# A fused decoder block: where the sums of the down projection's weights are made

## The chip, the cores and the metric

The kernel runs on one core of one Trainium2 chip. The metric is the device time of one launch in microseconds. The kernel before took 697.74, 702.74 and 703.54 us in three runs, median 702.74 us. One further execution was profiled. It took 699.71 us, and its span from the first to the last instruction is 697.9 us.

## What is computed

One layer of a residual decoder block, with 512 tokens of width 1024, everything in float32. `h` is a gained RMS norm of `x`, modulated by columns of `c_act @ ada_w`.

```python
h = rms_norm(x, norm1_g) * (1 + scale1) + shift1
q, k, v, p, g_attn, g_pool = split(h @ w_in)
attn = moba_attention(rms_norm(q), rms_norm(k), v, rel_bias)      # 8 heads of 64
pool = multiscale_pool(p) ...                                     # windows 2, 4, 8, 16
merged = sigmoid(g_attn) * (attn @ w_branch_attn) + sigmoid(g_pool) * (pool @ w_branch_pool)
x = x + gate1 * (merged @ w_out)
h2 = rms_norm(x, norm2_g) * (1 + scale2) + shift2
u = causal_dwconv(h2 @ w_up, conv_w, conv_b)
u_g, u_v = split(u)
x = x + gate2 * ((silu(u_g) * u_v) @ w_down)                      # w_down is 2816 x 1024
```

## The kernel before, in words

**Precision.** Each float32 operand of a large product is split into a high part, rounded by ScalarE (`hi_of`, L114), and a low part, a subtraction on VectorE (L124). Three matmuls (`mm3`, L133 to L135; `more`, L139 to L141) stand for one product.

**Stages, in order.** (1) `x` is normed and transposed. The columns of `ada_w` come as 512 KB tiles and are summed with `c` (`ada_sum`, L207). For each of eight 128-wide slices k of the width, the p and q projections accumulate `h_k` into eight banks of PSUM (`mm3s`, L146 and L149). Slice k needs two ada tiles, summed, and half of a tile of p and of q weights. (2) The k and v projections (`tok_proj`). (3) The norms of q and k, the transposes (`stacks`, L550) and per head the attention, with the sixteen gate projections filled in between (`gate_stream`). (4) The branches and `w_out`, then the second norm per token tile (`out_norm`). (5) The up projection, 22 channel pairs j, each with its convolution, SiLU and product on ScalarE and VectorE. (6) The down projection.

**Down by seven products.** The down projection multiplies 2x2 blocks with seven products instead of eight. It needs four blocks of `w_down` as they are (b11, b12, b22, b21) and four sums of them: t1 = b11 + b12, t3 = b12 + b22, t2 = b22 + t1, t4 = b21 + t2 (or an equal order of additions). The sums are made per tile kk of 128 channels by 512 columns, kk from 0 to 10, and are kept in DRAM tiles `tsum`. The seven phases of down read plain blocks and sums in the order b11, t1, t2, b21, t3, b22, t4. They are loaded by SP as units of two tiles kk each (`plan`, `load_unit`, L82).

**Two ways to make a sum tile.** `t_get`, `t_do` and `t_put` load the four blocks, add them by four instructions on VectorE (L773 to L776) and store the four sums. `t_step(kk, n)` makes them without a compute engine, in six steps n: GpSimd's queue (POOL) issues two plain loads into tiles `ta` and `tc` (n = 0, L794), then DMAs that accumulate another block into them (L789) and DMAs that store the running sum to `tsum` (L790). That is 11 DMAs of 256 KB a tile, seven of them from `w_down`, four of them stores. A step waits for the landing of the step before. All of these tiles come from the pool `wsum`, which has four buffers of 128x512.

**What sets the order.** PE, VectorE and ScalarE run in the order in which the program is written (`manual_schedule(engines=ENG)`). POOL and SP are not in that list: their instructions are placed by the scheduler of the language, which puts them as early as the buffers and the data let it. Each queue then runs in order. A POOL instruction that waits for a landing holds everything behind it on POOL: the `pow` of the norms (L324, L520, L198), the loads of the attention bias (L578), the low parts of `w_out` (L220) and the loads and stores of the residual (L927, L946, L1270).

**The sums before.** Tiles kk 0 to 3 are written into the attention loop, by `t_steps(2 * h, 0, range(4))` and its twin, one new tile every three steps. Tile 4 is loaded by `t_get(4)` in the loop over `out_norm` and added by VectorE at j = 0 of up. Tiles 5 to 10 are written into up, one step per j (`t_steps(j, 1, range(5, 11))`).

Of the kernel before, what the change touches and what calls it, by code (L numbers as in the profile page):

```python
# [32 lines left out]
NU = (NP // 2 + 1) // 2  # L33
# [22 lines left out]
def block_kernel(tc, x, cvec, ada, wtok, wch, pool_w, wbr, wout, wup, wdn, pack, table, out):  # L56
    nc = tc.nc
# [3 lines left out]
    with ctx:  # L61
# [692 lines left out]
        def t_tile(name):  # L754
            return tp_.tile([P, 512], F32, tag="t", name=name)

        def t_load(kk):
            i, u = divmod(kk, 2)
            b = {}
            for nm in ("b11", "b12", "b22", "b21"):  # L760
                b[nm] = t_tile(f"{nm}_{kk}")
                nc.gpsimd.dma_start(b[nm], wdn[plain[nm], i][:, u * 512 : u * 512 + 512])
            return b

        tb = {}

        def t_get(kk):
            tb[kk] = t_load(kk)

        def t_do(kk):  # L770

# [44 lines left out]
        gg = gate_stream()  # L816
        fill(gg, FIRST)
        share = (NG * 5.2 - FIRST) / H
        def t_steps(n, start, kks):

            for x_, kk in enumerate(kks):
                if 0 <= n - start - 3 * x_ < 6:
                    t_step(kk, n - start - 3 * x_)

        for h in range(H):
            pt = flip(h, rows)
            if h + 1 < H:
                rows = softmax(h + 1, *logits(h + 1))
            if h + 2 < H:
                bias_rows(h + 2)  # L830
            t_steps(2 * h, 0, range(4))
            fill(gg, 3)
            if h % 2 == 0 and h < 6:
                stacks(h // 2 + 1, False)
            elif h in (1, 3):
                stacks((h + 3) // 2, True)
            values(h, *pt)
            ada_col(2, h)
            if h == 5:
                pooling(3)  # L840
            if h == 6:
                pool_proj(3)

            t_steps(2 * h + 1, 0, range(4))
            fill(gg, 3 if h < 5 else (share - 3) / 2)
            if h < 5:
                ada_col(3, h)
            fill(gg, (share - 3) / 2)
# [89 lines left out]
        def out_norm(t):  # L938
            row = [xr[t, 0], xr[t, 1]]
            rs = rms_rows(row, f"y{t}")  # L940
            for f in range(2):
                n_ = slot(f"xn2_{t}_{f}")
                nc.vector.tensor_scalar(n_, row[f], rs, None, op0=ALU.mult)
                xn2[t, f] = n_
                x2d[t, f] = dpool.tile([P, 512], F32, name=f"x2d_{t}_{f}")
                nc.gpsimd.dma_start(x2d[t, f], row[f])  # L946

        for t in range(TT):
            for f in range(2):
                if (t, f) == (0, 0):  # L950
                    for t_ in range(2):
                        for f_ in range(2):
                            out_mm(t_, f_, 0, KT - 2)
                if (t, f) != (3, 0):
                    out_mm(t, f, KT - 2 if t < 2 else 0, KT)
                    out_post(t, f, ops[t, f])
                if late:
                    ada_col(4, late.pop(0))
                    if not late:
                        nc.vector.scalar_tensor_tensor(acol[:, 32:40], acol[:, 32:40], 1.0, pk[:, C_N2 : C_N2 + 8],  # L960
                                                       op0=ALU.add, op1=ALU.mult)
            out_norm(t)
            if t == 2:
                out_mm(3, 0, 0, KT)
                out_post(3, 0, ops[3, 0])
                flip_h2(1)
                t_get(4)

# [226 lines left out]
        for j in range(NP):  # L1197
            if j + 1 == NP:
                steps = [lambda: ahead("b11_0", 0), lambda: ahead("b11_0", 1)]
            else:  # L1200
                steps = [] if j < PLAIN else (prep_seven if j + 1 in SEVEN else prep_two)(j + 1)
            if j < 2:
                u = first[2 * j][1], first[2 * j + 1][1]
                if j == 0:
                    t_do(4)
                    t_put(4, nc.gpsimd)
                behind(0)
                if j == 1:
                    for st in prep_two(PLAIN):
                        st()  # L1210
                behind(1)
                h_forms(j)
            elif j in SEVEN:
                mine = [steps[0], lambda: behind(0), lambda: behind(1), steps[1]]
                u = seven(j, lambda n: mine[n]())
            else:
                if j < PLAIN:
                    for e in range(2):
                        upw[j, e] = ready.pop(f"up{2 * j + e}")
                u = [bank(f"u_{2 * j + e}") for e in range(2)]  # L1220
                for st in steps[:-1]:
                    st()
                up_mm(u[0], upw.pop((j, 0)), 0, S)
                behind(0)
                for st in steps[-1:]:
                    st()
                up_mm(u[1], upw.pop((j, 1)), 0, S)
                behind(1)
                if j in (2, 3):
                    h_forms(j)  # L1230
            pend.append((j, *u))
            t_steps(j, 1, range(5, 11))
            if j in ADA_AT:
                ada_col(5, ADA_AT[j])
        behind(0)
# [30 lines left out]
        def fetch(m, f):  # L1266
            for p in range(2):
                t = 2 * m + p
                x2[t, f] = slot(f"x2r_{t}_{f}")
                nc.gpsimd.dma_start(x2[t, f], x2d[t, f])  # L1270


# [4 lines left out]
        def step(acc, p, u, a, w, c0, c1, stop):  # L1277
            ac = slice(u * 256 + p * P, u * 256 + p * P + P)
            cs = slice(u * 512 + c0, u * 512 + c1)
            more(accs[acc][p][:, c0:c1], a[0][:, ac], a[1][:, ac], w[0][:, cs], w[1][:, cs],  # L1280
                 (acc, p) not in fresh, stop)
            fresh.add((acc, p))

        for n, (an, bn, acc) in enumerate(phases):
            last = n == len(phases) - 1
            held_ = []
            for i in range(NU):
                if n == 0 and i == 0:
                    ahead("b11_0", 3)
                w = unit(f"{bn}_{i}")  # L1290
                a = forms.pop((an, i))
                if last and i >= NU - 2:
                    held_.append((a, w, width(i) // 512))
                else:
                    for u in range(width(i) // 512):
                        for p in range(2):
                            step(acc, p, u, a, w, 0, 512, i == NU - 1 and u == width(i) // 512 - 1)
                if n == 0:
                    if i == 0:
                        s_forms(NU - 2)  # L1300
                    if i == 2:
                        s_forms(NU - 1)
                    split_s = fa["s2", i]
                    forms["s2", i] = split_act(split_s, f"s2_{i}", width(i) // 2)
                elif n == 1:
                    forms["a12", i] = split_act(fa["a12", i], f"a12_{i}", width(i) // 2)
                elif n == 2:
                    split_a("s3", i)
                    s2 = fa.pop(("s2", i))
                    nc.vector.tensor_add(s2, s2, fa.pop(("a12", i)))  # L1310
                    fa["s4", i] = s2
                elif n == 3:
                    split_a("s4", i)
                    split_a("a22", i)
            if last:
                for p in range(2):
                    for x_, (a, w, nu) in enumerate(held_):
                        for u in range(nu):
                            step(acc, p, u, a, w, 0, 512, x_ == len(held_) - 1 and u == nu - 1)
                    finish(p, 1, 0, "X")  # L1320
            if n == 0:
                keep("s1", "X")
            elif n == 1:
                keep("s5", "Y")
            elif n == 2:
                keep("s2", "X")
                fetch(0, 0)
            elif n == 3:
                for p in range(2):
                    finish(p, 0, 0, "Z", plus="s1")  # L1330
                fetch(1, 1)
            elif n == 4:
                for p in range(2):
                    finish(p, 1, 1, "X", minus=("s5", None))
                fetch(0, 1)
            elif n == 5:
                for p in range(2):
                    finish(p, 0, 1, "Y", minus=(None, "s2"))
                fetch(1, 0)
# [69 lines left out]
```

## Time and profile before

| what | value |
|---|---|
| median of three runs | 702.74 us (697.74 to 703.54) |
| the profiled execution | 699.71 us, span 697.9 us |
| PE busy, matmuls | 668.3 us, 96% of the span, 3403 |
| VectorE busy | 545.7 us, 78% |
| ScalarE busy | 367.1 us, 53% |
| POOL busy | 151.5 us, 22% |
| DMA | 139.37 MB, mean 200 GB/s; SP's queue 98.23 MB, POOL's queue 40.54 MB |
| mean granted clock of TensorE | 0.980 |

How to read it: an engine's busy time is the union of its instructions, with DMA-issuing ones of POOL shown where the view lists them. [...] A row of the timeline merges like instructions that follow each other (x4). The bracket at its end is the idle time of the engine before it, and what ended that. "PEclk" is the share of full speed that TensorE was granted.

### The profile page before, as it was taken

To read this page: it belongs to the slowest core of one execution; us is meant where nothing else is said; L and a number is where in the kernel's file an instruction comes from. 1 tells how busy PE (TensorE), PEld (TensorE's weight loads), DVE (VectorE), ACT (ScalarE), POOL (GpSimd) and SP (SyncE) were. 2 spreads that over 40 slices of the span, in tenths; PEclk is the share of its full clock that TensorE was granted. 3 is DMA by queue.
4 is the path that set the end of the run, shared out by engine and by line. 5 is a ranking of instruction groups with operands and counts; after the bars stand their busy time and mean duration, and the time that the engine had idled before them with its cause. 6 is when DMAs were issued, how large, how long until landed. Compare 5 with 4: busy or idle time off the path is not lost.

```text
span 697.9 us, 9445 instructions
## 1 busy us (share of the span) xinstructions
PE 668.3 (96%) x3403; PEld 567.0 (81%) x3403; DVE 545.7 (78%) x914; ACT 367.1 (53%) x631; POOL 151.5 (22%) x199
## 2 busy tenths in 40 slices
PE   7787898899999999999999999999999999999997
PEld 5565676788888888788899898889998888788886
DVE  5645697588887868887758999999898996978774
ACT  6423624466756446560364565565565563867440
POOL 5324073400000004561303434442000000001000
PEclk9989999899999999999999999999999999999999
DMA  8999769344445245769336999998334352566751
GB/s 316 336 344 338 235 170 292 113 135 136 137 162 184 96 147 122 260 216 336 142 102 199 226 289 246 309 251 245 107 121 151 76 180 81 183 229 230 291 194 60
DMA packets 44100, 139.37 MB, mean 200 GB/s; under 512 B 5795, under 2 KB 5964, under 8 KB 44054
## 3 DMA queue, kind: packets, MB, share of 16 engines
q1 hardware_dynamic: 28358, 98.23, 41.5%
q0 software_dynamic: 15696, 40.54, 22.2%
q8 instruction: 26, 0.43, 0.3%
q14 instruction: 20, 0.16, 0.1%
HBM read 123.00 MB, written 15.76 MB: 199 GB/s over the span
## 4 chain that ended last, share of the span: by engine, by line
PE 73%; DVE 5%; ACT 2%; issue 1%; POOL 0%; DMA 0%; DVEq 0%
PE u L133 7%; PE u L134 7%; PE u L135 7%; PE gate_ps L135 4%; PE gate_ps L134 4%; PE gate_ps L133 4%; PE X L141 2%; PE X L140 2%; PE X L139 2%; PE uX L141 2%; PE uX L139 2%; PE uX L140 2%; PE o L135 2%; PE o L133 2%; PE o L134 2%; PE Y L140 1%
## 5 line engine op out<-in xcount | busy, mean ns | idle before, releaser
L133 PE MATMUL u<-h2h,hi_up 128*128 128x512 f32 (+1 forms) x256 | 93.0, 363 | 0.0
L134 PE MATMUL u<-h2l,hi_up 128*128 128x512 f32 (+1 forms) x256 | 92.9, 363 | 0.0
L135 PE MATMUL u<-h2h,lo_up 128*128 128x512 f32 (+1 forms) x256 | 92.8, 362 | 0.0
L207 DVE CUSTOM_DVE_ANT_0 raw_ada<-raw_ada,cbc,pk 128x1024 f32<-128x1024 f32 x48 | 62.2, 1302 | 11.3 <-DMA raw_ada<-in_ada 9.5
L135 PEld LDWEIGHTS u<-h2h,lo_up 128*128 128x128 f32 x256 | 48.3, 189 | 7.6
L133 PEld LDWEIGHTS u<-h2h,hi_up 128*128 128x128 f32 x256 | 48.4, 189 | 7.3
L134 PEld LDWEIGHTS u<-h2l,hi_up 128*128 128x128 f32 x256 | 48.4, 189 | 7.2
L133 PE MATMUL gate_ps<-h_h,hi_gate 128*128 128x512 f32 x128 | 50.0, 390 | 0.0
L135 PE MATMUL gate_ps<-h_h,lo_gate 128*128 128x512 f32 x128 | 50.0, 390 | 0.0
L134 PE MATMUL gate_ps<-h_l,hi_gate 128*128 128x512 f32 x128 | 49.9, 390 | 0.0
L789 POOL DMA_DIRECT2D tc<-in_wdn x30 | 27.8, 928 | 26.6 <-DMA tc<-in_wdn 22.2
L124 DVE TENSOR_TENSOR lo_t<-raw_t,hi_t 128x1024 fp32r<-128x1024 f32 (+1 forms) x24 | 26.7, 1132 | 8.0 <-ACT hi_t L114 7.9
L114 ACT ACTIVATE hi_t<-raw_t 128x1024 fp32r<-128x1024 f32 (+1 forms) x24 | 23.7, 987 | 17.5 <-PE Y L141 8.4
L114 ACT ACTIVATE hi_up<-raw_up 128x1024 fp32r<-128x1024 f32 x28 | 29.2, 1050 | 4.3 <-PE u L134 4.3
L220 POOL TENSOR_TENSOR wo_l<-raw_wo,wo_h 128x512 fp32r<-128x512 f32 x16 | 25.6, 1620 | 20.3 <-ACT wo_h L219 16.5
L1083 DVE TENSOR_TENSOR lo_up<-raw_up,hi_up 128x1024 fp32r<-128x1024 f32 x22 | 26.7, 1220 | 2.9 <-ACT hi_up L114 2.9
L135 PEld LDWEIGHTS gate_ps<-h_h,lo_gate 128*128 128x128 f32 x128 | 24.0, 188 | 5.1
L133 PEld LDWEIGHTS gate_ps<-h_h,hi_gate 128*128 128x128 f32 x128 | 24.0, 188 | 4.6
L134 PEld LDWEIGHTS gate_ps<-h_l,hi_gate 128*128 128x128 f32 x128 | 24.0, 188 | 4.5
L605 ACT ACTIVATE L<-L,mn 128x512 f32<-128x512 f32 (+3 forms) x32 | 17.6, 552 | 19.2 <-DVE mn L601 19.2
L133 PE MATMUL o<-wo_h,mg_h 128*128 128x512 f32 x64 | 25.0, 391 | 0.0
L135 PE MATMUL o<-wo_h,mg_l 128*128 128x512 f32 x64 | 24.9, 389 | 0.0
(365 smaller groups left out, 2009.5 us busy)
## 6 DMA issues: line engine op xcount, KB each, us to landing
raw_ada<-in_ada SPq DMA_DIRECT2D x48, 512.0 KB, 5.4
raw_up<-in_wup SPq DMA_DIRECT2D x44, 512.0 KB, 5.5
tc<-in_wdn POOLq DMA_DIRECT2D x40, 256.0 KB, 6.6
raw_t<-tsum_t SPq DMA_DIRECT2D x20, 512.0 KB, 4.5
raw_gate<-in_wch SPq DMA_DIRECT2D x16, 512.0 KB, 4.3
ta<-in_wdn POOLq DMA_DIRECT2D x30, 256.0 KB, 6.8
raw_b<-in_wdn SPq DMA_DIRECT2D x15, 512.0 KB, 4.2
tsum_t<-ta POOLq DMA_DIRECT2D x20, 256.0 KB, 5.8
```

The costliest lines, as they stand in the source:

```text
L114: nc.scalar.activation(hi, raw, AF.Copy)
L124: nc.vector.tensor_sub(lo, raw, hi.bitcast(F32))
L133: nc.tensor.matmul(ps, sh, mh, start=start, stop=False)
L134: nc.tensor.matmul(ps, sh, ml, start=False, stop=False)
L135: nc.tensor.matmul(ps, sl, mh, start=False, stop=stop)
L139: nc.tensor.matmul(ps, sh, mh, start=start, stop=False, skip_group_check=True)
L140: nc.tensor.matmul(ps, sh, ml, start=False, stop=False, skip_group_check=True)
L141: nc.tensor.matmul(ps, sl, mh, start=False, stop=stop, skip_group_check=True)
L207: nc.vector.tensor_tensor_reduce(out=raw, in0=raw, in1=cbc, op0=ALU.mult, op1=ALU.add, scale=1.0, scalar=col(C_AB + i), accum_out=acol[:, ...
L220: (eng or nc.vector).tensor_sub(lo[:, :w], src, hi[:, :w].bitcast(F32))
L789: add = lambda to, nm: nc.gpsimd.dma_start(to, wdn[plain[nm], i][:, us], accum_op=ALU.add)
L1083: nc.vector.tensor_sub(lo, raw, hi.bitcast(F32))
```

## The change

The sums of tiles 0 to 3 leave the attention loop, and `t_steps` is gone. Tile 0 takes the way that tile 4 had (loads, four additions on VectorE, stores). Its loads are called behind `out_norm(3)`, and each is held by a one-column copy on GpSimd that writes into the buffer from `rss[7]`, the reciprocal root of the last token tile's norm: a load may not overwrite its buffer before that copy, and the copy needs the last norm. The four buffers of `wsum` go round, so all later tiles follow tile 0. Tiles 1 to 10 are made by accumulating DMAs in up, two steps per j instead of one, a new tile every three steps. The additions of tile 0 stand behind `h_forms(0)` at j = 0, where those of tile 4 stood ahead of it.

Two smaller edits go with it. The residual tiles that the end of down reads back (`x2r`) come from `wsum` instead of the large pool of slots. The split of the sums s2 into high and low parts comes two units later: those of units 0 to 3 at units 2 to 5 of the first phase of down, those of units 4 and 5 in the second phase.

```diff
-        def t_load(kk):
+        def t_load(kk, behind_):
             ...
                 b[nm] = t_tile(f"{nm}_{kk}")
+                nc.gpsimd.tensor_copy(b[nm][:, :1], behind_)
                 nc.gpsimd.dma_start(b[nm], wdn[plain[nm], i][:, u * 512 : u * 512 + 512])
...
-        def t_get(kk):
-            tb[kk] = t_load(kk)
+        def t_get(kk, behind_):
+            tb[kk] = t_load(kk, behind_)
...
-        def t_steps(n, start, kks):
-
-            for x_, kk in enumerate(kks):
-                if 0 <= n - start - 3 * x_ < 6:
-                    t_step(kk, n - start - 3 * x_)
-
         for h in range(H):
...
-            t_steps(2 * h, 0, range(4))
             fill(gg, 3)
...
-            t_steps(2 * h + 1, 0, range(4))
             fill(gg, 3 if h < 5 else (share - 3) / 2)
...
             rs = rms_rows(row, f"y{t}")
+            rss[4 + t] = rs
...
             out_norm(t)
+            if t == 3:
+                t_get(0, rss[7])
             if t == 2:
...
                 flip_h2(1)
-                t_get(4)
...
-                if j == 0:
-                    t_do(4)
-                    t_put(4, nc.gpsimd)
                 behind(0)
...
                 h_forms(j)
+                if j == 0:
+                    t_do(0)
+                    t_put(0, nc.gpsimd)
...
-            t_steps(j, 1, range(5, 11))
+            for n in (2 * j - 2, 2 * j - 1):
+                for kk in range(1, 11):
+                    if 0 <= n - 3 * (kk - 1) < 6:
+                        t_step(kk, n - 3 * (kk - 1))
...
-                x2[t, f] = slot(f"x2r_{t}_{f}")
+                x2[t, f] = t_tile(f"x2r_{t}_{f}")
...
+        def split_s(i):
+            forms["s2", i] = split_act(fa["s2", i], f"s2_{i}", width(i) // 2)
...
-                    split_s = fa["s2", i]
-                    forms["s2", i] = split_act(split_s, f"s2_{i}", width(i) // 2)
+                    if i > 1:
+                        split_s(i - 2)
                 elif n == 1:
+                    if i < 2:
+                        split_s(NU - 2 + i)
```

The order of POOL's queue tells where the scheduler puts these instructions. The first place is the start of the kernel. `rs_x` are the norms of `x`, which the first transposes need.

```order
 L170 DMA pk<-in_pack 128x262
-L794 DMA ta_1293<-in_wdn 128x512
-L794 DMA tc_1294<-in_wdn 128x512
-L794 DMA ta_1516<-in_wdn 128x512
-L794 DMA tc_1517<-in_wdn 128x512
 L324 ISA
 L324 TENSOR_TENSOR rs_x_172<-ms_x_170,mhalf 128x1
 L324 TENSOR_TENSOR rs_x_182<-ms_x_180,mhalf 128x1
-L789 DMA ta_1293<-in_wdn 128x512
 L324 TENSOR_TENSOR rs_x_214<-ms_x_212,mhalf 128x1
 L324 TENSOR_TENSOR rs_x_223<-ms_x_221,mhalf 128x1
-L789 DMA tc_1294<-in_wdn 128x512
```

Although they are written into the attention loop, the first sums stood at the very start of POOL's queue, ahead of the norms of `x`; with the change none of them is left there.

The second place is POOL's queue before the norm of k (`hr_k` are its reciprocal roots, `fd` the bias table; `b_4` are the loads of tile 4).

```order
-L762 DMA b_4_3293<-in_wdn 128x512
-L762 DMA b_4_3295<-in_wdn 128x512
-L790 DMA tsum_t_1_102<-tc_2048 128x512
 L231 DMA fd<-f_635 8x512
 L231 DMA fd<-f_636 8x128
-L762 DMA b_4_3297<-in_wdn 128x512
 L520 TENSOR_TENSOR hr_k_905<-hs_k_902,mhalf 128x8
 L520 TENSOR_TENSOR hr_k_912<-hs_k_909,mhalf 128x8
```

The last load of tile 4, which needs the buffer that the store of `tc_2048` frees, stood just ahead of the four roots of k; with the change only the two small stores of the bias table are ahead of them.

The third place is POOL's queue behind the last norm, with the change alone.

```order
L198 TENSOR_TENSOR rs_y_3276<-ms_y_3274,mhalf 128x1
L762 COPY b_0_3286<-rs_y_3276 128x1
L762 COPY b_0_3289<-rs_y_3276 128x1
L762 COPY b_0_3292<-rs_y_3276 128x1
L762 COPY b_0_3295<-rs_y_3276 128x1
L763 DMA b_0_3286<-in_wdn 128x512
L763 DMA b_0_3289<-in_wdn 128x512
L763 DMA b_0_3292<-in_wdn 128x512
L763 DMA b_0_3295<-in_wdn 128x512
L784 DMA tsum_t_0_83<-b_0_3286 128x512
```

Four copies and four loads now follow `rs_y`; the stores behind them wait for VectorE's additions, and the first `ta` of the accumulating tiles comes behind those stores, as it did before, now with ten tiles to go instead of six.

## The prediction, made before the changed kernel ran

> **What bounds the kernel now.** I read the page, then what PE waited for, then PE's timeline where those waits are, then the DMA of that stretch. The engine that sets the end is PE, and it loses its time early:
>
> ```profile
> span 697.9 us, 9445 instructions
> PE p L146 <- ACT h_h L403: 7.1, 2, 3.7
> PE T_True L550 <- DVE n_k L528: 4.8, 1, 4.8
> PE p L149 <- DVE h_l L408: 3.4, 1, 3.4
> PE p L146 <- ACT h_h L401: 3.0, 2, 1.7
> PE X L140 <- DVE lo_b L124: 1.0, 2, 0.6
> ```
>
> These are PE's waits over the whole span (us, times, longest). Nearly all lie in the p and q projections and at the first transpose of attention. From there to down PE waits for nothing worth a row. So whatever the change takes from the attention loop proper is worth nothing, and what it does to the first 130 us and to up decides.
>
> ```profile
> 18.02 1.20 PE L146 MATMUL p<-h_h,p0h 128*128 128x512 f32 x4
> 26.51 2.08 PE L146 MATMUL p<-h_h,p0h 128*128 128x512 f32 x4 [1.75 <-ACT h_h L401]
> 40.37 2.07 PE L149 MATMUL p<-h_l,hi_p 128*128 128x512 f32 x4 [3.44 <-DVE h_l L408]
> 56.26 1.74 PE L146 MATMUL p<-h_h,hi_p 128*128 128x512 f32 x4 [3.67 <-ACT h_h L403]
> 72.49 1.20 PE L146 MATMUL p<-h_h,hi_p 128*128 128x512 f32 x4 [3.45 <-ACT h_h L403]
> 83.33 1.07 PE L149 MATMUL q<-hi_q,h_l 128*128 128x512 f32 x4
> 84.24 1.07 PE L149 MATMUL q<-lo_q,h_h 128*128 128x512 f32 x4
> 85.15 0.39 PE L133 MATMUL k<-hi_k,h_h 128*128 128x512 f32 x1
> ```
>
> The block of p and q runs from 18.02 to 85.15, 67.1 us. Four matmuls at full pace take 0.91 us (83.33 to 84.24); the block has 48 such groups (8 slices, p and q, three each), 43.7 us. The excess is 23.4 us: the waits shown, and the slow stretch behind each (2.07 and 2.08 us for a group instead of 1.07).
>
> ```profile
> 33.21 1.06 ACT L114 ACTIVATE hi_p<-raw_p 128x1024 fp32r<-128x1024 f32 x1 [5.25 <-DMA raw_p<-in_wtok]
> 53.51 1.06 ACT L114 ACTIVATE hi_p<-raw_p 128x1024 fp32r<-128x1024 f32 x1 [9.20 <-DMA raw_p<-in_wtok]
> 69.73 1.06 ACT L114 ACTIVATE hi_p<-raw_p 128x1024 fp32r<-128x1024 f32 x1 [8.86 <-DMA raw_p<-in_wtok]
> 10.00:72.00 62.00, 47.08 (x185) 36.73 (x185) 34.20 (x60) 22.78 (x41) 22.16 (x34) 0.86 1.05 338
> q1 hardware_dynamic: 4317, 15.28, 55.7%
> q0 software_dynamic: 3504, 8.52, 45.3%
> raw_p<-in_wtok SPq DMA_DIRECT2D x4, 512.0 KB, 12.8
> raw_k<-in_wtok SPq DMA_DIRECT2D x4, 512.0 KB, 4.5
> ```
>
> Behind PE's waits stands ScalarE, which waits for weight tiles. From 10 to 72 us the DMA engines are full (share 1.05, 338 GB/s, granted clock 0.86). The two queue rows are the DMA view of the first 72 us: SP's loads (q1) take 55.7% of the engines' time, POOL's (q0) 45.3%. Those 8.5 MB are the sums of down's weights, which stand at the head of POOL's queue and are not wanted for 500 us. A tile of p takes 12.8 us to land there; a tile of k, issued mostly when POOL was quiet, 4.5.
>
> **Part by part. (a) The start.** Ahead of the first p matmul go four tiles of x, two of ada and those of p and q. Among them POOL issues four sum loads of 256 KB: 1.05 MB at 338 GB/s is 3.1 us. I take 2.5 us off the first matmul, to 15.5 (bounds 1 and 3.1).
>
> **(b) The p and q block.** Between the landings of two p tiles (33.2, 53.5, 69.7: 20.3 and 16.2 us) SP moves six tiles, 3.1 MB, 9.3 us at 338 GB/s; PE needs 10.9 us for them (12 groups). Without POOL's share the bytes alone no longer bind. What is left is SP's ring of five buffers, freed in VectorE's order:
>
> ```profile
> 38.42 1.29 DVE L207 CUSTOM_DVE_ANT_0 raw_ada<-raw_ada,cbc,pk 128x1024 f32<-128x1024 f32 x1 [2.89 <-DMA raw_ada<-in_ada]
> 43.68 0.33 SPq L82 DMA_DIRECT2D raw_p<-in_wtok  x1
> 60.25 0.33 SPq L82 DMA_DIRECT2D raw_p<-in_wtok  x1
> ```
>
> The second of these p tiles was issued 10.5 us after the first landed, some 3.5 of it VectorE waiting for ada tiles, and flew 9.8 us; the third 6.7 and 9.5. With 7 us and a flight of 5 they land some 12 us apart: 23 (13 tiles, 6.9 MB, at 338 GB/s, and the first latency), 35, 47. PE wants the second at 15.5 + 4 x 5.45 = 37.3, and a tile is usable 2.75 us after landing (53.51 to 56.26): 37.8. So about one wait of 1 to 3 us stays, with a slow stretch of 1.7 behind it, and some tenths early; I leave 5 us of the 23.4 and take 18.4 off (bounds 11.4, half of it, and 23.4).
>
> [...]
>
> **(c) The first transpose of attention.**
>
> ```profile
> 113.07 0.17 DVE L518 TENSOR_SCALAR hs_k<-hs_k 128x8 f32<-128x8 f32 x1
> 121.03 0.57 POOL L762 DMA_DIRECT2D b<-in_wdn  x1 [3.42 <-DMA tsum_t<-tc]
> 121.61 6.47 POOL L520 TENSOR_TENSOR hr_k<-hs_k,mhalf 128x8 f32<-128x8 f32 x4
> 117.91 1.22 DVE L124 TENSOR_TENSOR lo_v<-raw_v,hi_v 128x1024 fp32r<-128x1024 f32 x1
> 124.17 1.09 PE L550 MATMUL T_True<-pk,n_q 128*128 128x128 f32 x4 [4.83 <-DVE n_k L528]
> 119.00:129.00 10.00, 5.17 (x17) 4.04 (x16) 3.05 (x6) 0.68 (x1) 7.96 (x7) 0.66 0.53 188
> ```
>
> VectorE has the first sums of k at 113.2, but POOL, held by tile 4's last load, starts the roots at 121.6. Started at 113.2 the first is ready at 114.9, all four (1.6 us each) by 119.7; VectorE is free for `n_k` at 119.1, PE resumes near 120 instead of 124.2. That is 4.2 us, and the slow stretch behind (clock 0.66 over these ten us), eight matmuls at half pace and the transpose, about 1.9: together 6.1 (bounds 4.0, the wait alone, and 6.8, no wait left).
>
> **(d) Up.** The ten tiles now beside up issue 110 DMAs where six issued 66. What that costs PE can be read from up itself, which had 114 us with sums and then none:
>
> ```profile
> 440.00:480.00 40.00, 40.00 (x254) 36.39 (x253) 36.31 (x55) 23.51 (x41) 16.26 (x24) 1.00 1.00 272
> 500.00:540.00 40.00, 40.00 (x250) 36.21 (x249) 35.68 (x54) 22.60 (x39) 0.00 (x0) 1.00 0.35 113
> L1083 DVE TENSOR_TENSOR lo_up<-raw_up,hi_up x19: 1216/1219/1227, 380.1 to 558.5; 128x1024 fp32r<-128x1024 f32 x19
> ```
>
> With full DMA engines (share 1.00) PE ran 254 matmuls in 40 us, with idle ones (0.35) 250, and VectorE's subtraction takes 1216 to 1227 ns in both. So 70 us more of such traffic cost nothing; SP's loads of `w_up` cover it, as they are issued well ahead of PE. Bounds: nothing, and 4 us if a `w_up` tile is once late (the size of a wait in (b)). VectorE's additions for one tile are four in either kernel. Ahead of them now stand four copies and four loads on POOL:
>
> ```profile
> POOL tsum_t L783 <- DVE b L773: 18.0, 1, 18.0
> ```
>
> POOL sat idle 18.0 us there, from the last norm to VectorE's first sum; four copies of no more than a root's 1.6 us each and a flight of 4 to 10 us fit into it.
>
> **(e) Down.** PE's two waits for `lo_b` (1.0 us) come in the first phase, where VectorE also splits s2; two of those splits leave its front. I take 0.5 us off; bounds 1.0, and 1 us lost where the second phase now has two more. `x2r` in `wsum` frees after the stores of the last sums; its readers are tens of us later: nothing.
>
> **Sum.** 2.5 + 18.4 + 6.1 + 0 + 0.5 = 27.5 us off the profiled execution's 699.71: 672 us. The other runs of before are up to 4 us longer, the median 3, so I say 673. Bounds: 34 us off gives 665 (664 with the spread of the runs), 11 us off (1 + 11.4 + 4.0 - 4 - 1) gives 688.
>
> **Rivals.** *The sums come too late* (slower). The place is SP's in-order queue, which reaches the last load of t1, the one that tile 10 feeds, at 603.67:
>
> ```profile
> 376.49 0.54 POOL L794 DMA_DIRECT2D ta<-in_wdn  x1 [1.01 <-DMA tsum_t<-b]
> 406.62 0.77 POOL L794 DMA_DIRECT2D ta<-in_wdn  x1
> 439.62 0.57 POOL L794 DMA_DIRECT2D ta<-in_wdn  x1 [0.84 <-DMA tsum_t<-ta]
> 487.94 0.58 POOL L790 DMA_DIRECT2D tsum_t<-tc  x1 [5.33 <-DMA tc<-in_wdn]
> 603.67 0.32 SPq L82 DMA_DIRECT2D raw_t<-tsum_t  x1
> ```
>
> Two tiles go at a time, a new pair every 30 to 33 us, the last store 48 us after the last pair began. Five pairs end near 379 + 4 x 32 + 50 = 557 (all less the 27 us gained, as is the deadline); tile 10's t1, the third of six steps, at most half of its 50 us into the chain, near 532. Spare: 72 us, 18 a pair. Above 50 us a pair PE would wait in down, from 57 longer than it gained; at 70 by 80 us: 672 + 80 = 752. [...] 4%.
>
> [...]
>
> *Only the waits at attention go.* The ring and VectorE's order, not POOL's share, space the p tiles: (b) is worth 6 us or less. For it: 7 to 10 us from a landing to the next issue. Against: flights of 10 us where a quiet queue has 4.5. 1 + 6 + 6 off: 687. 14%.
>
> *It does not do what it says.* The scheduler could have put the tiles elsewhere; the order rows show none before the last norm. 699 to 703, 4%.
>
> **How the numbers follow.** Forecast 78%, partial gain 14%, no change 4%, late sums 4%. One per cent, 7 us, is about what a measurement of this kernel can tell. Forecast and partial are both beyond it: faster 0.92, same 0.04, slower 0.04. Range 664 to 688: the forecast's bounds, which take in the partial case's middle.
>
> **What would show it.** Right: from 10 to 60 us no POOL DMA, p tiles landing near 23, 35 and 47 us, the first k matmul near 64 instead of 85; `hr_k` starting with the sums of k and a wait at T_True of about 1 us; in up a full DMA share until about 530 (557 less the gain) and no PE wait; the last store over 30 us before SP's first t1 load needs it. Wrong: k still starting after 75, or PE idle in down behind `raw_t`.

## The result, and the profile after

The changed kernel takes 667.01 us in the median of six runs (665.74 to 668.03). The kernel before took 702.11 us in the median of six runs beside them (697.74 to 703.54). The ratio is 0.951, with a 95% interval from 0.948 to 0.954: 35 us faster. The two profiled executions are 32.2 us apart: 699.71 us before, 667.53 us after.

Of what PE waits for over the whole span, the waits in the p and q block and at the first transpose of attention, the kernel after (us, times, longest):

```profile
span 665.6 us, 9452 instructions
PE p L146 <- ACT h_h L403: 1.3, 2, 0.9
PE T_True L550 <- DVE n_k L528: 0.5, 1, 0.5
```

The waits at p for `h_l` and for the first form of `h_h` are gone, the other two have shrunk from 7.1 to 1.3 us and from 4.8 to 0.5. To see where the time went stage by stage, take the first start of a stage's matmuls. Each row gives the durations (min/median/max, ns), and behind the comma the first and the last start in us. Neighbours overlap: the first k matmuls of the kernel after are shown 0.39 us long and start 0.23 us apart. The kernel before:

```profile
L133 PE MATMUL k<-hi_k,h_h x32: 389/389/499, 85.1 to 109.0; 128*128 128x512 f32 x32
L133 PE MATMUL gate_ps<-h_h,hi_gate x128: 387/389/477, 141.9 to 259.0; 128*128 128x512 f32 x128
L133 PE MATMUL u<-h2h,hi_up x256: 277/389/396, 350.5 to 585.9; 128*128 128x512 f32 x96, 128*128 128x256 f32 x32
L139 PE MATMUL X<-hi_b,a_h x22: 388/389/397, 586.6 to 602.5; 128*128 128x512 f32 x22
```

The kernel after:

```profile
L133 PE MATMUL k<-hi_k,h_h x32: 389/390/499, 61.0 to 84.8; 128*128 128x512 f32 x32
L133 PE MATMUL gate_ps<-h_h,hi_gate x128: 387/390/478, 111.4 to 227.8; 128*128 128x512 f32 x128
L133 PE MATMUL u<-h2h,hi_up x256: 278/390/397, 319.3 to 554.8; 128*128 128x512 f32 x96, 128*128 128x256 f32 x32
L139 PE MATMUL X<-hi_b,a_h x22: 388/390/390, 555.4 to 570.2; 128*128 128x512 f32 x22
```

With the first p matmul (18.02 and, below, 14.50) and the two spans, the differences of neighbours make a table:

| stretch | before | after | gained | term of the sum |
|---|---|---|---|---|
| start to first p matmul | 18.0 | 14.5 | 3.5 | (a) 2.5 |
| p and q block | 67.1 | 46.5 | 20.6 | (b) 18.4 |
| k, v, first transposes, to the first gate matmul | 56.8 | 50.4 | 6.4 | (c) 6.1 |
| attention to the end of `w_out` | 208.6 | 207.9 | 0.7 | none |
| up | 236.1 | 236.1 | 0.0 | (d) 0 |
| down | 111.3 | 110.2 | 1.1 | (e) 0.5 |

All but 1.8 us of the gain lies in the first 112 us. (In a second profile of the changed kernel, the last run below, the k matmuls start at 59.8 us instead of 61.0; so about 1 us at this place can be chance.) The block itself in PE's timeline, after:

```profile
14.50 1.19 PE L146 MATMUL p<-h_h,p0h 128*128 128x512 f32 x4
38.31 1.21 PE L146 MATMUL p<-h_h,hi_p 128*128 128x512 f32 x4 [0.86 <-ACT h_h L403]
49.94 1.21 PE L146 MATMUL p<-h_h,hi_p 128*128 128x512 f32 x4 [0.41 <-ACT h_h L403]
61.00 0.39 PE L133 MATMUL k<-hi_k,h_h 128*128 128x512 f32 x1
```

ScalarE's roundings of the p tiles, after. The second and third start as their tiles land; ScalarE was busy when the first landed:

```profile
21.76 1.04 ACT L114 ACTIVATE hi_p<-raw_p 128x1024 fp32r<-128x1024 f32 x1
35.56 1.06 ACT L114 ACTIVATE hi_p<-raw_p 128x1024 fp32r<-128x1024 f32 x1 [4.29 <-DMA raw_p<-in_wtok]
47.18 1.06 ACT L114 ACTIVATE hi_p<-raw_p 128x1024 fp32r<-128x1024 f32 x1 [4.25 <-DMA raw_p<-in_wtok]
```

The tiles land near 21, 35.5 and 47 us (33, 53.5 and 70 before; 23, 35 and 47 predicted). The short waits of 0.86 and 0.41 us have no slow stretch behind them: the group of four takes 1.21 us. The queues in the first 72 us (packets, MB, share of 16 engines), after:

```profile
q1 hardware_dynamic: 5606, 19.32, 76.1%
q0 software_dynamic: 48, 0.13, 0.5%
raw_p<-in_wtok SPq DMA_DIRECT2D x4, 512.0 KB, 7.9
```

POOL's 8.52 MB are gone and SP moves 19.3 MB in the same time, where it had moved 15.3. Behind the block, POOL's roots of k and the first transpose, after:

```profile
89.18 7.29 POOL L520 TENSOR_TENSOR hr_k<-hs_k,mhalf 128x8 f32<-128x8 f32 x4 [4.37 <-DVE hs_k L518]
95.72 0.63 PE L550 MATMUL T_True<-pk,n_q 128*128 128x128 f32 x4 [0.53 <-DVE n_k L528]
```

POOL now waits for VectorE's sums, not the sums for POOL, and the four transposes take 0.63 us instead of 1.09. In up, the stretches with the ten tiles (busy time of PE, its weight loads, VectorE, ScalarE, POOL; granted clock, DMA share, GB/s), after:

```profile
410.00:460.00 50.00, 50.00 (x301) 44.83 (x301) 46.10 (x70) 29.42 (x50) 20.11 (x29) 1.00 1.00 273
460.00:510.00 50.00, 50.00 (x330) 46.11 (x329) 43.80 (x65) 27.89 (x50) 20.54 (x30) 1.00 0.98 274
```

PE is busy without a gap beside full DMA engines. The sums reach their reader in time: POOL stores t1 of tile 10 at 508.69, and the sixth load of `raw_t`, the one that reads it, is issued at 571.3, within the merged row of SP's twelve loads. The very last store, that of t4 of tile 10, is issued at 538.60. After:

```profile
508.69 0.54 POOL L791 DMA_DIRECT2D tsum_t<-ta  x1 [1.44 <-DMA ta<-in_wdn]
538.60 0.56 POOL L791 DMA_DIRECT2D tsum_t<-tc  x1 [2.97 <-DMA tc<-in_wdn]
548.39 34.15 SPq L82 DMA_DIRECT2D raw_t<-tsum_t  x12
```

### The profile page after: what moved, and what is told of

The parts are those of the page before. It is cut to its first block, busy times and chain, and to the rows that moved or that the text cites. A ratio compares the mean times of both kernels' runs of the same rounds, so it can differ in the third digit from the quotient of the medians.

```text
span 665.6 us, 9452 instructions
## 1 busy us (share of the span) xinstructions
PE 655.8 (99%) x3403; PEld 559.5 (84%) x3403; DVE 544.6 (82%) x914; ACT 366.8 (55%) x631; POOL 154.0 (23%) x203
## 4 chain that ended last, share of the span: by engine, by line
PE 81%; DVE 11%; DMA 3%; ACT 2%; issue 2%; SPq 0%; DVEq 0%; ACTq 0%
PE u L133 8%; PE u L135 8%; PE u L134 8%; PE gate_ps L134 4%; PE gate_ps L135 4%; PE gate_ps L133 4%; DMA raw_p<-in_wtok 3%; DVE raw_ada L207 3%; PE X L141 2%; PE X L139 2%; PE X L140 2%; PE uX L141 2%; PE uX L140 2%; PE uX L139 2%; PE o L135 2%; PE o L133 2%
## 5 line engine op out<-in xcount | busy, mean ns | idle before, releaser
L790 POOL DMA_DIRECT2D tc<-in_wdn x30 | 27.5, 926 | 31.6 <-DMA tc<-in_wdn 27.5
```

The costliest lines, as they stand in the source:

```text
L790: add = lambda to, nm: nc.gpsimd.dma_start(to, wdn[plain[nm], i][:, us], accum_op=ALU.add)
```

## The experiments

My theory after the result: the 8.5 MB of sums at the head of POOL's queue took DMA bandwidth from SP's weight loads (terms a and b); the last load of tile 4 held the roots of k on POOL (term c); and beside up the same traffic costs nothing. Rivals: POOL's in-order queue and not the bandwidth made the start late; the sums cost time wherever they stand beside attention, so the gain is one of attention; the small edits carry part of it; and the sums in up are near to being late. Each group of runs has its own runs of the kernel before beside it, with medians of 699.75, 702.50 and 702.89 us, so ratios to it are given with the times.

**Sums beside attention proper.**

```diff
  # the kernel before, in t_step, n == 0
+                 if kk < 2:
+                     for b in tb[kk]:
+                         nc.gpsimd.tensor_copy(b[:, :1], kr[3][:, :1])
                  for t, nm in zip(tb[kk], ("b11", "b12")):
```

> The kernel before, with its sums of tiles 0 to 3 still beside attention, but held back by a one-column copy from the last root of k, so that none of them stands at the head of POOL's queue or ahead of the roots of k. My theory (it is the start and the roots that gained, not attention itself): the p and q block as in the changed kernel, first k matmul near 61 us instead of 85, T_True near 95, and a time of 667 to 670 us, within 3 us of the changed kernel. The rival that the sums cost something wherever they stand beside attention: 672 us or more. In this version no sum moves into up, so a time below the changed kernel's by over 2 us would say that the ten tiles in up do cost something.

Measured: 679.02 us, ratio 0.971 (0.969 to 0.973). The start is as the theory has it (first k matmul 59.8), but the time is 12 us above the changed kernel's: my number failed, the rival's held. VectorE's largest wait and PE's, in this run:

```profile
DVE L L601 <- DMA trev<-fd: 12.3, 2, 7.1
PE gate_ps L133 <- DVE mn L601: 5.9, 1, 5.9
```

`trev` is the attention bias of a head. POOL loads it, here behind steps of the sums:

```profile
102.98 1.07 POOL L789 DMA_DIRECT2D tc<-in_wdn  x1
107.70 0.58 POOL L790 DMA_DIRECT2D tsum_t<-ta  x1 [3.64 <-DMA ta<-in_wdn]
108.26 0.57 POOL L578 DMA_DIRECT2D trev<-fd  x1
```

The changed kernel issues the first two of these loads at once after the roots of k:

```profile
96.42 1.20 POOL L578 DMA_DIRECT2D trev<-fd  x2
```

So beside attention the sums do cost something, though no sum of the kernel before lay there: its POOL queue had stored the last of them by 121 us. Up answers the other question. In this run it has six accumulating tiles, in the changed kernel ten, and both take the same 236 us (329.6 to 565.8 here):

```profile
L133 PE MATMUL u<-h2h,hi_up x256: 278/389/396, 329.6 to 565.1; 128*128 128x512 f32 x96, 128*128 128x256 f32 x32
L139 PE MATMUL X<-hi_b,a_h x22: 388/389/398, 565.8 to 581.7; 128*128 128x512 f32 x22
```

**The same, with the bias loads on SP's queue.** It asks whether the 12 us come from POOL's order or from the traffic.

```diff
  # the run above, in bias_rows
-            nc.gpsimd.dma_start(
+            nc.sync.dma_start(
```

> The first experiment (sums of tiles 0 to 3 beside attention, behind the last root of k; 679 us, with VectorE waiting 12.3 us for the attention bias) with one line changed: the eight loads of the bias go through SP's queue instead of POOL's. If the 10 us that it lost against the changed kernel come from POOL's queue, where the bias loads stood behind the steps of the sums: 667 to 671 us, and PE's wait of 5.9 us at the first gate matmul gone. If they come from the DMA traffic beside attention: 675 or more. A bias load may also be held on SP by the ring of weight tiles; then the wait moves, and the time lies between.

Measured: 669.11 us, ratio 0.952 (0.949 to 0.956). The wait at the first gate matmul is gone, and up begins at 319.9, as in the changed kernel:

```profile
L133 PE MATMUL u<-h2h,hi_up x256: 278/389/396, 319.9 to 555.4; 128*128 128x512 f32 x96, 128*128 128x256 f32 x32
```

The sums still flow beside attention: in the four slices of the page from 117 to 184 us the DMA engines move 230 to 306 GB/s, against 64 to 184 in the changed kernel. What is left against the changed kernel is 2 us, of which about one belongs to the small edits, which this kernel doesn't have. So 10 of the 12 us were POOL's order, and the traffic beside attention cost about 1.5 us: from the first gate matmul (110.5) to up this run takes 209.4 us, the changed kernel 207.9.

**The old chain put back, unused.** This kernel does extra work that nothing reads.

```diff
  # the changed kernel, in the attention loop, two steps per head
+            d_steps(2 * h)          # t_step for four tiles, stores to unused DRAM tiles
```

> The changed kernel, with the old chain of four tiles put back as unused copies: the same 44 DMAs of 256 KB in the attention loop, which the scheduler hoists to the head of POOL's queue, with results that nothing reads. The real sums stay where the change put them. My theory: the p and q block is stretched again to about 67 us with p tiles landing 16 to 20 us apart, first k matmul near 85, and the time goes back by 20 to 27 us, to 687 to 694 (the wait at T_True came from tile 4's loads, which are not put back, so the time does not return all the way to 702). The rival that the start was bound by SP's ring and VectorE's order: within 10 us of the changed kernel.

Measured: 693.41 us, ratio 0.991 (0.989 to 0.993): 26 us of the 35 lost again. PE's first wait is to the tenth that of before, and the first k matmul starts at 85.4:

```profile
PE p L146 <- ACT h_h L403: 7.1, 2, 3.7
...
L133 PE MATMUL k<-hi_k,h_h x32: 389/389/499, 85.4 to 109.2; 128*128 128x512 f32 x32
```

**The same chain with an eighth of the bytes.**

```diff
-        def d_step(kk, n, w=512):
+        def d_step(kk, n, w=64):
```

> The kernel with the unused copies, each DMA cut from 128x512 to 128x64: the same 44 instructions on POOL, the same waits of step on step, one eighth of the bytes (32 KB instead of 256 KB). My theory (bandwidth: SP's loads share the DMA engines with POOL's): the loss nearly goes, 667 to 671 us, first k matmul near 62. The rival that what hurts is POOL's queue, held in order behind landings (the roots of x and of h wait behind it): close to the run with the full copies, 685 or more. Halfway would mean that the number of descriptors counts, not the bytes, since their number is the same.

Measured: 669.26 us, ratio 0.957 (0.955 to 0.959). POOL's queue over the first 72 us and k's start:

```profile
q0 software_dynamic: 3664, 1.55, 14.5%
L133 PE MATMUL k<-hi_k,h_h x32: 389/389/499, 61.8 to 85.7; 128*128 128x512 f32 x32
```

The packets are as many as before (3664 against 3504). The instructions on POOL and their order are those of the full chain, and each step still waits for the landing before it, though not as long. Only the bytes are fewer (1.55 MB against 8.52), and with them 24 of 26 us of the loss are gone. Nor has POOL's order anything to hold back there: with the full chain the last root of `x` runs on POOL at 12.6 us, behind a wait for VectorE's sum and not for a DMA, and from there to the roots of q at 86.6 us POOL runs only DMAs and the clearing of a buffer (`kz`), which the p and q block doesn't read. The start is lost to bytes, not to POOL's order or to the number of packets.

**Half of the tiles at the start.**

```diff
  # the changed kernel: tiles 1 and 2 in the attention loop, 3 to 10 in up
+            early_steps(2 * h)
...
-                for kk in range(1, 11):
+                for kk in range(3, 11):
```

> The changed kernel, with two of its accumulating tiles (1 and 2) put back into the attention loop, from where the scheduler hoists them to the head of POOL's queue: half of the four that stood there. The p and q block then shares the DMA engines with 22 DMAs, 5.8 MB, instead of 44, to about 40 us. By bandwidth, my theory: about half of the 24 us that the full copies cost, 8 to 14 us, 675 to 681, with late p tiles in the first half of the block and none after 45 us. A rival, by which the first wait starts the loss and the ring does not recover: 688 or more. A rival by which SP's ring absorbs half the traffic: 670 or less.

Measured: 685.89 us, ratio 0.976 (0.972 to 0.981). My number was 5 us too low, and the time lies between my range and the rival's 688.

```profile
q0 software_dynamic: 2448, 5.90, 31.3%
L133 PE MATMUL k<-hi_k,h_h x32: 389/389/499, 78.9 to 102.7; 128*128 128x512 f32 x32
```

I had taken these two tiles for half of the early traffic and let them end at 40 us. But on shared engines the last of their stores is issued at 50.7 us; and of the old chain's four tiles only 8.52 MB fell into the first 72 us, so that these are 5.90 of 8.52 (0.13 MB of each are another load). The k matmul comes 17.9 us late with 5.8 MB too much and 24.4 us late with 8.4: 3.1 and 2.9 us a MB, close to the 3.0 us that a MB takes at 338 GB/s. The narrow chain's 1.4 MB made it 0.8 us late, or 2.0 against the other profile of the changed kernel, too little to tell whether the first MB is cheaper. Nor does the ring stay behind, as the rival has it: the last two p tiles land at 52.6 and 63.9 us, 11.3 us apart, as in the changed kernel (11.6).

**These two tiles held to the middle of the block.**

```diff
  # the run above, in t_step, n == 0
+                if kk < 3:
+                    for b in tb[kk]:
+                        nc.gpsimd.tensor_copy(b[:, :1], hh[4][:, :1].bitcast(F32))
```

> The run with two tiles back at the start (686 us), with one line more: their first loads are held by a copy from the high part of h's slice 4, which stands in the middle of the p and q block, near 37 us. The same 22 DMAs, 5.8 MB, now flow from about 37 to 75 us instead of from 2 to 56. My theory, that early traffic costs its time on full DMA engines only while SP's loads have no lead: the start and the first half of the block as in the changed kernel, the last p tile some microseconds later, the rest absorbed by the lead that k and v weights have: 668 to 675 us. The rival that every MB on POOL's queue in the first 72 us costs its 3 us wherever it stands: 683 to 687.

Measured: 676.48 us, ratio 0.964 (0.961 to 0.966), 1.5 us over my range and under the rival's 683 to 687. But that number of the rival let all 5.8 MB flow in the first 72 us. By then POOL's queue had moved 4.0 MB, 3.9 of them sums, and at 3 us a MB these give about 679. So the time alone doesn't decide between the two; the stages have to. POOL's queue over the first 72 us, the last p tile's rounding, which starts as the tile lands, PE's wait at p, and PE's wait behind the block with the microsecond of clock that follows it (third from the end):

```profile
q0 software_dynamic: 1656, 4.01, 21.9%
50.76 1.06 ACT L114 ACTIVATE hi_p<-raw_p 128x1024 fp32r<-128x1024 f32 x1 [8.04 <-DMA raw_p<-in_wtok]
...
PE p L146 <- ACT h_h L403: 5.1, 2, 4.2
...
84.06 1.24 PE L229 MATMUL fp<-hot,rel 33*8 33x512 f32 x4 [1.32 <-DVE n_q L528]
86.00:87.00 1.00, 1.00 (x4) 0.76 (x3) 1.00 (x2) 0.00 (x0) 0.00 (x0) 0.50 1.01 410
```

The last p tile lands 3.6 us later than in the changed kernel. Up to 51 us POOL's queue had moved 1.1 MB of sums, so here too a MB cost about its 3 us. Behind the wait PE runs at half clock until 58.7 us (granted clock 0.58 in the mean from 52 to 60 us), and k starts at 66.9, 5.9 us late. The 2.1 MB that POOL's queue moved from there (51 us) to k's start made PE wait for no load, which fits the theory. They weren't free altogether: by the start of up another 3 us are lost, PE's wait of 1.3 us for `n_q` and a stretch at half clock behind it, from 86.0 to 89.4. VectorE was 2 us behind with `n_q`, from a wait for ScalarE, which had itself waited 3.3 us for `pwr`, a 256 KB load of SP.

**Tile 4 alone.**

```diff
  # the kernel before, in t_load for tile 4
+                nc.gpsimd.tensor_copy(b[nm][:, :1], rs_last[0])
                 nc.gpsimd.dma_start(b[nm], wdn[plain[nm], i][:, u * 512 : u * 512 + 512])
...
+            rs_last[:] = [rs]       # in out_norm: the root of the norm
```

> The kernel before, with one thing changed: the four loads of tile 4 are held by one-column copies from the last norm of q, k and the residual that has run when they are called, so that they no longer stand ahead of the roots of k on POOL. The sums of tiles 0 to 3 stay at the head of POOL's queue. This is term (c) alone. My theory: the p and q block as before (first k matmul near 85), the wait at T_True down from 4.8 us to about 1, and 5 to 7 us less than before. The run with the full copies, 6.3 us under before with that term and the small edits, says the same. The rival that the roots of k were late for another reason: within 1 us of before.

Measured: 695.93 us, ratio 0.990 (0.987 to 0.994): 6.6 us less than before, in the middle of what was expected, with an interval of 4 to 9. The roots of k start right behind the small stores of the bias table, and PE's wait is 1.0 us:

```profile
115.63 0.56 POOL L792 DMA_DIRECT2D tsum_t<-tc  x1 [4.27 <-DMA tc<-in_wdn]
...
117.22 2.10 POOL L520 TENSOR_TENSOR hr_k<-hs_k,mhalf 128x8 f32<-128x8 f32 x1
...
PE T_True L550 <- DVE n_k L528: 1.0, 1, 1.0
```

The roots still don't start with VectorE's first sums, at 113.1: a store of the early tiles, 115.63, stands ahead of them and waits 4.27 us for a landing. From the first k matmul (85.0) to the first gate matmul (138.0) this run takes 53.0 us, against 56.8 before and 50.4 with the change. So the profile gives tile 4's loads 3.8 us of term (c)'s 6.4; the rest went only where the early sums were gone too. This run is not the whole of term (c), as its expectation had it.

**The small edits undone.**

```diff
-                x2[t, f] = t_tile(f"x2r_{t}_{f}")
+                x2[t, f] = slot(f"x2r_{t}_{f}")
...
-                    if i > 1:
-                        split_s(i - 2)
+                    split_s(i)
...
-                    if i < 2:
-                        split_s(NU - 2 + i)
```

> The changed kernel with its two smaller edits undone: the residual tiles of the end of down back in the pool of slots, the split of the sums s2 back at its old place in the first phase of down. My theory: 0.5 us slower than the changed kernel (between 1 us faster and 1.5 slower), with PE's two waits for lo_b back (about 1 us). The rival that these edits carry a good part of the gain: 3 us slower or more.

Measured: 668.08 us (667.05 to 669.03), ratio 0.955 (0.953 to 0.957), against 667.01 and 666.17 in the two sets of runs of the changed kernel. The wait returns:

```profile
PE X L140 <- DVE lo_b L124: 1.0, 2, 0.6
```

The edits are worth about 1 us, at the upper end of what I took: in this profile down takes 111.3 us, as before, against 110.2 in the changed kernel.

**One tile at a time.** It makes the rival of late sums happen.

```diff
  # the changed kernel, in t_step, n == 0, and three steps per j
+                if kk > 1:
+                    for b in tb[kk]:
+                        nc.gpsimd.tensor_copy(b[:, :1], done[0][:, :1])
...
+                done[:] = [tb[kk][1]]          # at n == 4
...
-            for n in (2 * j - 2, 2 * j - 1):
...
+            for n in range(3 * j, 3 * j + 3):
+                if n < 60:
+                    t_step(n // 6 + 1, n % 6)
```

> The changed kernel, with its ten accumulating tiles made one after the other: the first loads of each tile are held by a copy from the finished tile ahead of it, so that no two tiles overlap. This makes the rival of sums that come too late happen. A tile alone should take 22 to 30 us (five landings of 4 to 6 us in a row). By my working of that rival the last t1 load of SP, near 572, is met up to some 23 us a tile; at 28 us a tile the third step of tile 10 ends near 352 + 9 x 28 + 14 = 618, and PE waits in down behind raw_t: 690 to 710 us. Should it stay within 2 us of the changed kernel, the spare in front of down is larger than I worked out.

Measured: 712.02 us, ratio 1.013 (1.008 to 1.018): slower than before. A first load every 28 to 34 us beside up, ScalarE waiting for the load of t1, and PE in the second phase of down:

```profile
402.24 0.56 POOL L800 DMA_DIRECT2D ta<-in_wdn  x1 [0.19 <-POOL tc L798]
...
433.26 0.56 POOL L800 DMA_DIRECT2D ta<-in_wdn  x1 [0.18 <-POOL tc L798]
...
626.63 0.63 ACT L114 ACTIVATE hi_t<-raw_t 128x512 fp32r<-128x512 f32 x1 [29.37 <-DMA raw_t<-tsum_t]
...
PE Y L139 <- ACT hi_t L114: 40.0, 2, 24.2
```

The store of t1 of tile 10 was issued at 612.9 (618 expected), after the point at which SP wants it. The mechanism and its place are as the rival had them; the price was 2 us above my range: 40.0 us of waiting, and some 5 us more, in which PE starts again at half pace behind each of the two long pauses (15.79 and 24.19 us; the matmuls behind them start 0.43 us apart instead of 0.23).

**The changed kernel again.**

> The changed kernel once more, unaltered, on the chip of the run beside it, so that small differences to it can be read: 665 to 669 us, and again no stretch of half clock behind the two short waits in the p and q block.

Measured: 666.17 us (665.86 to 666.46), ratio 0.948 (0.946 to 0.951), granted clock 0.999. None of the other kernels is faster.

## Why the prediction was right

It said 673 us, with 664 to 688 as its range; the median is 667.0, and the profiled gain 32.2 us where the sum had 27.5.

- **(a) The start**: 3.5 us instead of 2.5, just over the bound of 3.1, which was the time of the four sum loads that I counted. In the kernel before, a fifth of POOL's sum DMAs was issued at 8.9 us, also ahead of the first p matmul; I left it out. That the bytes are the cause is shown as in the block: the first p matmul starts at 18.2 us with the full unused chain and at 14.6 with the narrow one.
- **(b) The block**: the mechanism is shown by the narrow chain (bytes decide). The size was off by 2.2 us: I left 5 us of excess, a wait and a slow stretch of 1.7 behind it; 2.8 were left, with two waits of together 1.3 us and no slow stretch. The 5 us were more than my own figures gave: by the landings at 35 and 47 us the waits come to 0.5 us and 1.1. The ring and VectorE's order that I had set as the next limit are what is left: the p tiles land where I put them, and from 13 to 50 us SP waits 30.5 us for VectorE to free a buffer and 1.5 for a landing. The rival by which this ring, not POOL's share, spaces the tiles falls with the full and the narrow chain.
- **(c) The transposes**: 6.4 us in the profile, for 6.1. The hold by POOL's queue is shown, but I put all of it down to tile 4's last load. Alone that load is worth 3.8 us in the profile; a store of the early tiles held the roots as well. The sum holds because the change takes both away.
- **(d) Up**: 0.0 us. Reading the cost of the traffic from up itself, with and without it, was right to the tenth; the run with six tiles in up confirms it. It is the length of the stage that shows this. The counts of 254 and 250 matmuls in 40 us, which I also compared, mix matmuls of two widths.
- **(e) Down**: 1.1 for 0.5: both waits for `lo_b` went, and the second phase lost nothing.
- **Attention**: 0.7 us that no term had; the cause is open.
- **The spread**: I added 1 us because other runs of before were longer than the profiled one. The changed kernel has no such spread (665.7 to 668.0), so its median lies at the profiled time while that of before lies 2.4 us above.
- **The late sums**: the pairs came every 29 to 34 us (30 to 33 predicted). I put t1 of tile 10 at 505 (532 less 27), and it was stored at 508.7; its load at 571.3 (603.67 less 32.4). The full DMA share ended near 530, as I said. The last pair took longer than the 50 us that I gave it: its t4 was stored at 538.6, 10 us ahead of SP's first load of t1 at 548.4 and not the 30 that I asked of the last store. It cost nothing, as t4 is read in the last phase, and the last t1 stood 40 us ahead of that load. The 4% that I gave this rival are my estimate and stand on no run.

One statement of mine was too narrow: that what the change takes from the attention loop proper is worth nothing. For this change it is true, since no sum lay there; as a rule it is false, as the first experiment shows.

## What to carry to other kernels

Look up where a queue's order has put the transfers that a program writes elsewhere: these sums were written into the attention loop and stood in the first microseconds, where every MB cost about its own time on the DMA engines (2.9 to 3.1 us). A transfer with no near reader belongs into a stretch whose own loads run well ahead of their readers, and there it was free, at full DMA engines (up took 236 us with six tiles and with ten, at a DMA share of 0.98 to 1.00 from 410 to 510 us with ten). On a queue that issues in order, look for what stands behind the held instruction: the held roots of k cost some 6 us here, and the held bias loads 10, which were gained back when only these loads went to another queue beside the same traffic.

## What the runs showed of the hardware that I had not expected

I had read from the row at 26.51 of the kernel before that PE runs at half pace behind an idle time of 1.75 us. In the run with two tiles at the start the same place has the same idle time, and full pace:

```profile
26.42 1.19 PE L146 MATMUL p<-h_h,p0h 128*128 128x512 f32 x4 [1.73 <-ACT h_h L401]
```

One microsecond of each, with PE's granted clock third from the end, the kernel before:

```profile
27.00:28.00 1.00, 1.00 (x4) 0.71 (x4) 0.28 (x1) 0.96 (x2) 0.63 (x2) 0.50 1.05 430
```

and the run with two tiles at the start:

```profile
27.00:28.00 1.00, 1.00 (x6) 0.84 (x5) 0.34 (x1) 0.88 (x2) 0.63 (x2) 1.00 1.04 426
```

So the length of an idle time near 1.7 us does not by itself decide. Nor does a least length show: with the two held tiles, half clock begins at 86.0 us behind an idle time of 1.32 us, four small matmuls and three of k. In the trace of the kernel before, the low clock ahead of the last instructions comes in six stretches, four of 3.4 us and two of 6.8 (the row of the kernel before lies in the one from 25.96 to 29.38).

What decides is not shown: no run here moved a pause and left the rest as it was. The waits of 0.41 and 0.86 us in the p and q block after, and of 0.80 and 1.00 us there in the narrow chain's run, had no low clock behind them: a group of four took 1.20 or 1.21 us.
